# Split weights kept in DRAM for their second use, and an output stage whose transposes and projection share three PSUM tiles

## The chip, the cores and the metric

The kernel runs on one core of one Trainium2 chip. The metric is the device time of one execution in microseconds (us), the median of three runs. The core has five engines that the text names: TensorE (PE, with its weight loads as PEld), VectorE (DVE), ScalarE (ACT), GpSimd (POOL) and SyncE (SP). In this kernel SP issues every DMA, in one order. SBUF is the working memory on the chip, PSUM the memory that TensorE writes, DRAM the large memory behind the DMA engines.

## The reference, cut to what matters

One layer over 2048 tokens of width 1024. One projection of the normed input feeds three branches; each branch's output is multiplied by a gate, projected and merged with weights that are computed too.

```python
h = _layer_norm(x, ln_in_g, ln_in_b)
proj = h @ w_in[l]                       # 1024 x 7592
(a_q, a_k, a_v, a_gate, i_q, i_k, i_w, b_q, b_k, b_v, b_gate,
 c_q, c_gate, m_gate) = _split_cols(proj, IN_SPLITS)
# partial rotary embedding on a_q, a_k, i_q, i_k, b_q, b_k
o_a = _dsa_attention(a_q, a_k, a_v, i_q, i_k, i_w)     # top 256 keys by an indexer
y_a = (o_a * jax.nn.silu(a_gate)) @ w_proj_a[l]
o_b = _diff_attention(b_q, b_k, b_v, lam)
y_b = (o_b.reshape(bsz, seq, B_WIDTH) * jax.nn.silu(b_gate)) @ w_proj_b[l]
y_c = (o_c.reshape(bsz, seq, C_WIDTH) * jax.nn.silu(c_gate)) @ w_proj_c[l]   # o_c: attention into mem
g = jax.nn.sigmoid(m_gate.reshape(bsz, seq, N_BRANCH, D_MODEL))
merged = g[:, :, 0] * y_a + g[:, :, 1] * y_b + g[:, :, 2] * y_c
h = _layer_norm(DEEPNORM_ALPHA * h + merged @ w_out[l], ln_g[l], ln_b[l])
```

## The kernel before, in words

**Three products for one.** Every large product is made of three (`mm3`, L76 to L79): both operands are split into a rounded part H and the rest L, and TensorE adds H by H (L77), H by L (L78) and L by H (L79) in PSUM. `split` (L67 to L74) makes the parts: a copy into the rounded type, on GpSimd (L69) or ScalarE (L71), then a subtraction (L74) on GpSimd or VectorE.

**Two halves.** The 2048 tokens are 16 blocks of 128. The transposed, split input of 8 blocks (a half) fits into SBUF at a time, in `H4`. `save_hT` stores half 0's to DRAM (`ht_d`, four stores of 2 MB), and `reload` brings it back when half 1 is through. So every column group of `w_in` is needed twice, once for each half.

**The weights.** `load_win` (L227) loads 256 columns of `w_in` in raw pieces `wr` of 256 KB (L235; four for a group, two of 512 KB for the very first) and splits each piece into the tile `w` of 2 MB, of which there are two. `dense` (L240) and `gate_steps` (L253) call it, so it runs once for each half. `dense_ai01` (L266) does the same for 424 columns in two tiles; its copies are ScalarE's in half 0 and GpSimd's in half 1.

**The order in time.** Half 0: `aq`, `ai`, a first top-k over blocks 2 to 7 beside `bk`, `bv` and `bq`; its end runs into half 1's products. Then half 1's input, `aq`, `ai`, two more top-k groups, `bk`, `bv`, `bq`, and all 20 gate jobs (`JOBS`, L378) of half 1. H is reloaded; half 0's gate jobs follow: four at once, twelve spread as filler through the second attention (four heads of 16 blocks, keys `kg`, values `vg`, queries `bq`), four after it, beside the memory tokens' products. The first attention, the mixing of branches two and three, and the output stage come behind that.

**Work beside the weights.** GpSimd does the rotary steps (L138 to L141, on `do`, the copied product) and, at the end of a top-k group, a comparison for each block (L576, tile `ja`), on which VectorE's chain of scans (L579 to L582) waits. Both stand in GpSimd's order among the weight splits. SP issues raw pieces, stores of products and loads in one order; a DMA that has to wait for an engine holds up all behind it. Apart from a few places written out by hand, the order of each engine is set by a scheduler when the kernel is built.

**The output stage.** `stage1` (L1032) takes pairs of blocks. `gated` (L925) loads the gate `ys` (L927), transposes the first branch's output on TensorE into PSUM `gT` (L930), multiplies it by the gate on VectorE (L932), copies it on ScalarE (L933) and subtracts on GpSimd (L934). `branch` (L937) makes the projection from it, four PSUM tiles `yps` for a pair, which VectorE multiplies into `ft` (L943). `gT` has one PSUM tile, `yps` two, `ys` one buffer. The output projection (`fz`) runs between.

Of the kernel before, what the change touches and what calls it, by code (L numbers as in the profile page):

```python
# [58 lines left out]
def tile_layer(ctx, tc, x, mem, ln_in_g, ln_in_b, w_in, w_mem_kv, diff_lambda, diff_norm_g,  # L59
# [23 lines left out]
    def dram(name, shape, dt=F32):  # L83
        return dr.tile(shape, dt, name=name)
# [20 lines left out]
    mg_d = [dram(f"mg_d{p}", [128, KT, 256]) for p in range(NP)]  # L105

# [120 lines left out]
    def load_win(cols, eh=G, el=G, rpool=None):  # L227
        w = dw.tile([128, 2, KT, 256], F32R, name="w")
        n = sum(c for _, c in cols)
        m = 2 if rpool is None else 4  # L230
        for i in range(0, KT, m):
            raw = (rpool or dw).tile([128, m, 256], F32, name="wr", bufs=2)
            o0 = 0
            for c0, cn in cols:
                SP.dma_start(raw[:, :, o0:o0 + cn], w_view(w_in, i * 128, m, c0, cn))  # L235
                o0 += cn
            split(w[:, 0, i:i + m, :n], w[:, 1, i:i + m, :n], raw[:, :, :n], eh, el)
        return w
# [27 lines left out]
    def dense_ai01(half):  # L266
        W = []
        for i in range(2):
# [5 lines left out]
            W.append(w)  # L274
            for c0, cols in ((0, [(C_AK, 128), (C_IQ, 128)]), (256, [(C_IQ + 128, W_AI - 256)])):
                n = sum(c for _, c in cols)
                for k in (0, 2):
                    raw = dw.tile([128, 2, 256], F32, name="wr", bufs=2)
                    o0 = 0
                    for a0, an in cols:  # L280
                        SP.dma_start(raw[:, :, o0:o0 + an], w_view(w_in, i * 512 + k * 128, 2, a0, an))
                        o0 += an
                    split(w[:, 0, k:k + 2, c0:c0 + n], w[:, 1, k:k + 2, c0:c0 + n], raw[:, :, :n], A if half == 0 else G, G)
# [641 lines left out]
    def gated(pool, psp, pname, o, s, r, b, oT):  # L925
        t = slice(128 * (b % 2), 128 * (b % 2) + 128)
        SP.dma_start(s, sg_d[r][b // 4][:, :, 128 * (b % 4):128 * (b % 4) + 128])  # L927
        ps = psp.tile([128, 4, 128], F32, name=pname, bufs=2 if pname == "cps" else 1)
# [7 lines left out]
    def branch(psp, w, oT, u, t, bufs):  # L936
        y = psp.tile([128, 2, 256], F32, name="yps", bufs=bufs)  # L937
# [73 lines left out]
    for p in range(NP):  # L1011
        T = []
        for r, w, mix in ((1, wb, gated_b), (2, wc, gated_c)):
            oT = yp.tile([128, 2, 4, 256], F32R, name="yoT")
            mix(p, oT)
            for u in range(4):
# [3 lines left out]
                branch(yq, w, oT, u, t, 1)  # L1020
# [12 lines left out]
    def stage1(p, acc):  # L1033
        oT = fs.tile([128, 2, 4, 256], F32R, name="yoT")
        for b in (2 * p, 2 * p + 1):
            o = fs.tile([128, 512], F32, name="fo")
            SP.dma_start(o, oa_d[b])
            gated(fs, fqr, "gT", o, fs.tile([128, 4, 128], F32, name="ys", bufs=1), 0, b, oT)
        for u in range(4):
# [3 lines left out]
            branch(fqr, wa, oT, u, t, 2)  # L1043
# [129 lines left out]
```

## Time and profile before

| what | before |
| --- | --- |
| median of 3 runs | 2956.33 us (2955.36 to 2962.07) |
| profiled execution | 2954.62 us, of which 2952.8 are the span |
| TensorE busy | 2785.7 us (94%) |
| VectorE busy | 2130.6 us (72%) |
| ScalarE busy | 1398.0 us (47%) |
| GpSimd busy | 1140.0 us (39%) |
| moved by DMA | 383.09 MB, mean 130 GB/s |
| mean granted clock of TensorE | 0.980 |

The profiled execution is one of its own and not among the three. The span runs from the first to the last instruction. A share of busy time is a mean over the whole span; where an engine is short of work is seen in the stretches, and why in the waits. In rows of the trace, times are us from the start of the span; `out<-in` are the names of the tiles, and a bracket at a row's end is the idle time of the engine before it, with what ended it.

### The profile page before, as it was taken

What the parts mean: (1) busy time and instruction counts of PE and PEld (TensorE: products, weight loads), DVE (VectorE), ACT (ScalarE), POOL (GpSimd) and SP (SyncE); (2) the same over time, 40 slices, a digit from 0 to 9 for tenths busy, and PEclk for the clock granted to TensorE, in tenths of its full rate; (3) what the DMA queues carried; (4) which work ended last, traced back from release to release, by engine and by line L of the source; (5) the groups of instructions that cost most, each with busy time, mean ns of one, the idle gap of its engine ahead of it and who ended that gap; (6) DMA issues with size and microseconds to landing.
All of it is one profiled execution on the core that took longest, in us unless ns stands there. A gap on an engine that the chain in (4) does not pass through costs nothing.

```text
span 2952.8 us, 49447 instructions
## 1 busy us (share of the span) xinstructions
PE 2785.7 (94%) x17488; PEld 2494.6 (84%) x17488; DVE 2130.6 (72%) x4885; ACT 1398.0 (47%) x2716; POOL 1140.0 (39%) x1510
## 2 busy tenths in 40 slices
PE   6999989999999988999999998998999999987998
PEld 6899989987888867787888887897999899977887
DVE  7189988999668997577777773447777777774555
ACT  3266645773346860344444442436555655552010
POOL 7554566435433328344444435231222222211232
PEclk9999999999999999999999999999999999998999
DMA  9454444342322364433333325235333333358542
GB/s 341 134 149 143 148 121 136 119 144 93 115 86 84 95 196 143 134 96 104 107 109 96 109 68 153 71 98 185 101 104 98 116 111 110 116 169 271 185 146 83
DMA packets 357111, 383.09 MB, mean 130 GB/s; under 512 B 29952, under 2 KB 285312, under 8 KB 356352
## 3 DMA queue, kind: packets, MB, share of 16 engines
q1 hardware_dynamic: 356864, 379.94, 41.6%
q8 instruction: 138, 2.26, 0.3%
q14 instruction: 109, 0.89, 0.1%
HBM read 240.15 MB, written 139.69 MB: 129 GB/s over the span
## 4 chain that ended last, share of the span: by engine, by line
PE 57%; DVE 12%; DMA 6%; issue 5%; POOL 4%; ACT 3%; SPq 1%; DVEq 0%; POOLq 0%; ACTq 0%
PE dps L77 6%; PE dps L78 6%; PE dps L79 6%; PE ops L741 4%; DVE jd L531 4%; PE aops L886 4%; PE apt L881 3%; PE lg L636 3%; PE lg L637 3%; PE yps L78 3%; PE yps L77 3%; PE yps L79 3%; PE pt L749 2%; PE fz L79 2%; PE fz L78 2%
## 5 line engine op out<-in xcount | busy, mean ns | idle before, releaser
L77 PE MATMUL dps<-H,w 128*128 128x512 f32 x1280 | 519.3, 406 | 26.1 <-DMA H<-ht_d 8.1
L78 PE MATMUL dps<-H,w 128*128 128x512 f32 x1280 | 504.8, 394 | 0.0
L79 PE MATMUL dps<-H,w 128*128 128x512 f32 x1280 | 503.8, 394 | 0.9 <-POOL w L74 0.9
L69 POOL TENSOR_SCALAR w<-wr 128x512 fp32r<-128x512 f32 x240 | 184.9, 778 | 591.7 <-PE dps L79 449.7
L74 POOL TENSOR_TENSOR w<-wr,w 128x512 fp32r<-128x512 f32 (+2 forms) x254 | 361.1, 1431 | 17.2 <-ACT w L71 11.0
L77 PE MATMUL dps<-w,H 128*128 128x256 f32 (+1 forms) x1152 | 341.9, 298 | 12.9 <-POOL w L69 5.7
L544 ACT ACTIVATE ja<-sall,thr 128x1280 bf16<-128x1280 f32 (+4 forms) x224 | 302.1, 1348 | 109.0 <-DVE thr L540 99.1
L78 PE MATMUL dps<-w,H 128*128 128x256 f32 (+1 forms) x1152 | 342.8, 298 | 4.1 <-POOL w L74 4.1
L79 PE MATMUL dps<-w,H 128*128 128x256 f32 (+1 forms) x1152 | 341.4, 297 | 2.2 <-DVE H L74 2.2
L531 DVE TENSOR_SCALAR_CACHE_REDUCE jd<-sall,thr 128x1408 bf16<-128x1408 f32 (+6 forms) x231 | 330.9, 1433 | 6.4
L77 PEld LDWEIGHTS dps<-H,w 128*128 128x128 f32 x1280 | 243.4, 190 | 72.6 <-issue 13.9
L79 PEld LDWEIGHTS dps<-H,w 128*128 128x128 f32 x1280 | 242.6, 190 | 53.2 <-POOL w L74 1.8
L78 PEld LDWEIGHTS dps<-H,w 128*128 128x128 f32 x1280 | 244.1, 191 | 37.6
L639 DVE CUSTOM_DVE_ANT_0 AP<-lg,bias 128x512 f32<-128x512 f32 (+3 forms) x304 | 181.8, 619 | 124.6 <-PE lg L637 60.6
L504 DVE SCALAR_TENSOR_TENSOR sall<-ir,iw,sall 128x512 f32<-128x512 f32 (+3 forms) x266 | 212.8, 852 | 57.9 <-ACT ir L500 56.4
L77 PEld LDWEIGHTS dps<-w,H 128*128 128x128 f32 x1152 | 224.0, 195 | 16.4 <-POOL w L69 6.2
L71 ACT CAST apr<-apt 128x512 fp32r<-128x512 f32 (+1 forms) x288 | 157.5, 562 | 159.8 <-PE apt L881 128.3
L78 PEld LDWEIGHTS dps<-w,H 128*128 128x128 f32 x1152 | 224.5, 195 | 6.5 <-POOL w L74 5.8
L77 PE MATMUL yps<-yoT,H 128*128 128x256 f32 x768 | 223.5, 293 | 4.5 <-DVE ft L943 3.9
L74 DVE TENSOR_TENSOR apr<-apt,apr 128x512 fp32r<-128x512 f32 (+1 forms) x288 | 185.6, 656 | 58.2 <-ACT apr L71 56.4
L79 PEld LDWEIGHTS dps<-w,H 128*128 128x128 f32 x1152 | 224.3, 195 | 3.5 <-DVE H L74 2.6
L886 PE MATMUL aops<-apr,VA 128*128 128x256 f32 x1088 | 208.8, 299 | 16.9 <-ACT apr L71 6.7
(244 smaller groups left out, 6820.2 us busy)
## 6 DMA issues: line engine op xcount, KB each, us to landing
wr<-in_w_in_dram SPq DMA_DIRECT2D x220, 256.0 KB, 3.0
tm_d<-do SPq DMA_DIRECT2D x96, 256.0 KB, 2.1
bq<-qb_d SPq DMA_DIRECT2D x128, 128.0 KB, 3.3
aq<-qa_d SPq DMA_DIRECT2D x128, 128.0 KB, 3.2
yt<-tm_d SPq DMA_DIRECT2D x64, 256.0 KB, 3.1
sg_d<-do SPq DMA_DIRECT2D x48, 256.0 KB, 2.5
ys<-sg_d SPq DMA_DIRECT2D x48, 256.0 KB, 3.5
facc<-mg_d SPq DMA_DIRECT2D x48, 256.0 KB, 4.7
```

What stands on the lines that cost most here:

```text
L69: G.tensor_scalar(H, src, 1.0, 1.0, op0=ALU.mult, op1=ALU.mult)
L71: A.copy(H, src)
L74: el.tensor_tensor(L, src, H.bitcast(F32), op=ALU.subtract)
L77: PE.matmul(ps, lH, rH, start=start, stop=False)
L78: PE.matmul(ps, lH, rL, start=False, stop=False)
L79: PE.matmul(ps, lL, rH, start=False, stop=stop)
L504: V.scalar_tensor_tensor(s[:, c0:c0 + cn], r[:, :cn], iw[:, h:h + 1], s[:, c0:c0 + cn], op0=ALU.mult, op1=ALU.add)
L531: V.tensor_scalar(jd[:, :L], sc[b], t.bitcast(F32)[:, i:i + 1], None, op0=op, op1=ALU.add, accum_out=dst[:, i:i + 1])
L544: A.activation(ja[:, :L], sc[b], AF.Sign, bias=thr.bitcast(F32)[:, i:i + 1], scale=-1.0, accum_out=cnt[:, i:i + 1])
L639: V.tensor_tensor_reduce(P[:, c0:c0 + cn], ps[:, :cn], bias[:, c0:c0 + cn], scale=-0.125, scalar=-LOW, op0=ALU.add, op1=ALU.min, accum_out ...
L741: PE.matmul(o_ps.rearrange("p a d -> p (a d)"), pr[:, a, i], v, start=(k0 + i == 0 and a == 0), stop=(k0 + i == b and a == 1))
L886: PE.matmul(o_ps.rearrange("p a d -> p (a d)"), VA[:, k0 + i], pr[:, a, i].rearrange("p e q -> p (e q)"), start=(k0 + i == 0 and a == 0), ...
```

## The change

`load_win` keeps a table `w_d` by the first column of its group. On the first use the tile is made as before and then stored whole, with one DMA of 2 MB, to a DRAM tensor of its own. On the second use the tile is filled from there by one DMA of 2 MB; there are no raw pieces and no split. `dense_ai01` does this for its two tiles (1.7 MB each, stored in half 0, loaded in half 1). In the output stage `gT` and the projection's `yps` become one name with three PSUM tiles in turn, and `ys` has two buffers.

```diff
--- before.py
+++ after.py
@@ -103,6 +103,7 @@
     oa_d = [dram(f"oa_d{b}", [128, 512]) for b in range(NB)]
     ob_d = [dram(f"ob_d{b}", [128, 512]) for b in range(NB)]
     mg_d = [dram(f"mg_d{p}", [128, KT, 256]) for p in range(NP)]
+    w_d = {}
 
     const = ctx.enter_context(tc.tile_pool(name="const", bufs=1))
     idf = const.tile([128, 128], F32, name="idf")
@@ -226,6 +227,10 @@
 
     def load_win(cols, eh=G, el=G, rpool=None):
         w = dw.tile([128, 2, KT, 256], F32R, name="w")
+        key = cols[0][0]
+        if key in w_d:
+            SP.dma_start(w.bitcast(F32), w_d[key])
+            return w
         n = sum(c for _, c in cols)
         m = 2 if rpool is None else 4
         for i in range(0, KT, m):
@@ -235,6 +240,8 @@
                 SP.dma_start(raw[:, :, o0:o0 + cn], w_view(w_in, i * 128, m, c0, cn))
                 o0 += cn
             split(w[:, 0, i:i + m, :n], w[:, 1, i:i + m, :n], raw[:, :, :n], eh, el)
+        w_d[key] = dram(f"w_d{key}", [128, 2, KT, 256])
+        SP.dma_start(w_d[key], w.bitcast(F32))
         return w
 
     def dense(kind, half, cols, idx, w=None):
@@ -272,6 +279,9 @@
                 w = dw.tile([128, 2, KT, 256], F32R, name="w")
                 w = w.rearrange("p a k c -> p (a k c)")[:, :8 * W_AI].rearrange("p (a k c) -> p a k c", a=2, k=4)
             W.append(w)
+            if half:
+                SP.dma_start(w.bitcast(F32), w_d["ai", i])
+                continue
             for c0, cols in ((0, [(C_AK, 128), (C_IQ, 128)]), (256, [(C_IQ + 128, W_AI - 256)])):
                 n = sum(c for _, c in cols)
                 for k in (0, 2):
@@ -280,7 +290,9 @@
                     for a0, an in cols:
                         SP.dma_start(raw[:, :, o0:o0 + an], w_view(w_in, i * 512 + k * 128, 2, a0, an))
                         o0 += an
-                    split(w[:, 0, k:k + 2, c0:c0 + n], w[:, 1, k:k + 2, c0:c0 + n], raw[:, :, :n], A if half == 0 else G, G)
+                    split(w[:, 0, k:k + 2, c0:c0 + n], w[:, 1, k:k + 2, c0:c0 + n], raw[:, :, :n], A, G)
+            w_d["ai", i] = dram(f"w_dai{i}", [128, 2, 4, W_AI])
+            SP.dma_start(w_d["ai", i], w.bitcast(F32))
         for p in range(4 * half, 4 * half + 4):
             ps = [dqs.tile([128, 512], F32, name="dps") for _ in range(2)]
             for a in range(2):
@@ -925,7 +937,7 @@
     def gated(pool, psp, pname, o, s, r, b, oT):
         t = slice(128 * (b % 2), 128 * (b % 2) + 128)
         SP.dma_start(s, sg_d[r][b // 4][:, :, 128 * (b % 4):128 * (b % 4) + 128])
-        ps = psp.tile([128, 4, 128], F32, name=pname, bufs=2 if pname == "cps" else 1)
+        ps = psp.tile([128, 4, 128], F32, name=pname, bufs=2 if pname == "cps" else 3)
         for c in range(4):
             PE.transpose(ps[:, c], o[:, c * 128:(c + 1) * 128], idf)
         with tc.high_priority():
@@ -933,8 +945,8 @@
             A.copy(oT[:, 0, :, t], s)
             G.tensor_tensor(oT[:, 1, :, t], s, oT[:, 0, :, t].bitcast(F32), op=ALU.subtract)
 
-    def branch(psp, w, oT, u, t, bufs):
-        y = psp.tile([128, 2, 256], F32, name="yps", bufs=bufs)
+    def branch(psp, w, oT, u, t, name, bufs):
+        y = psp.tile([128, 2, 256], F32, name=name, bufs=bufs)
         for i in range(2):
             c = slice(256 * u + 128 * i, 256 * u + 128 * i + 128)
             for k in range(4):
@@ -1017,7 +1029,7 @@
                 t = yw.tile([128, 2, 256], F32, name="yt")
                 T.append(t)
                 SP.dma_start(t, tm_d[r][p // 2][:, 2 * u:2 * u + 2, 256 * (p % 2):256 * (p % 2) + 256])
-                branch(yq, w, oT, u, t, 1)
+                branch(yq, w, oT, u, t, "yps", 1)
         for u in range(4):
             G.tensor_tensor(T[u], T[u], T[4 + u], op=ALU.add)
             SP.dma_start(mg_d[p][:, 2 * u:2 * u + 2], T[u])
@@ -1035,12 +1047,12 @@
         for b in (2 * p, 2 * p + 1):
             o = fs.tile([128, 512], F32, name="fo")
             SP.dma_start(o, oa_d[b])
-            gated(fs, fqr, "gT", o, fs.tile([128, 4, 128], F32, name="ys", bufs=1), 0, b, oT)
+            gated(fs, fqr, "gT", o, fs.tile([128, 4, 128], F32, name="ys"), 0, b, oT)
         for u in range(4):
             t = fs.tile([128, 2, 256], F32, name="ft")
             SP.dma_start(t, tm_d[0][p // 2][:, 2 * u:2 * u + 2, 256 * (p % 2):256 * (p % 2) + 256])
             SP.dma_start(acc[u], mg_d[p][:, 2 * u:2 * u + 2])
-            branch(fqr, wa, oT, u, t, 2)
+            branch(fqr, wa, oT, u, t, "gT", 3)
             V.tensor_tensor(acc[u], acc[u], t, op=ALU.add)
 
     def accs(ap, bufs):
```

The lines of the changed program are some 12 further down than those of before behind this. In SP's order these are the pieces of ai's first and second tile in half 0, among stores of `aq` products (`qa_d`). Before:

```order
L225 DMA qa_d_0_85<-de 128x4x256
L281 DMA wr<-in_w_in_dram 128x2x168 x2
L225 DMA qa_d_1_86<-de 128x4x256
L225 DMA qa_d_2_87<-de 128x4x256
L225 DMA qa_d_3_88<-de 128x4x256
L281 DMA wr<-in_w_in_dram 128x2x128 x4
L281 DMA wr<-in_w_in_dram 128x2x168 x2
L235 DMA wr<-in_w_in_dram 128x2x256 x4
```

With the change (`w_dai` and `w_d` are the kept weights):

```order
L226 DMA qa_d_1_86<-de 128x4x256
L291 DMA wr<-in_w_in_dram 128x2x168
L226 DMA qa_d_2_87<-de 128x4x256
L226 DMA qa_d_3_88<-de 128x4x256
L291 DMA wr<-in_w_in_dram 128x2x128 x2
L295 DMA w_dai_1097<-w 128x3392
L291 DMA wr<-in_w_in_dram 128x2x128 x2
L291 DMA wr<-in_w_in_dram 128x2x168 x2
L240 DMA wr<-in_w_in_dram 128x2x256
L295 DMA w_dai_1118<-w_1099 128x3392
L240 DMA wr<-in_w_in_dram 128x2x256 x2
```

Stores of 1.7 MB (L295) stand between the pieces of the second ai tile and ahead of most pieces of the next group. Next, GpSimd at the end of the first top-k group (blocks 2 to 7, which runs into half 1's products), from the comparison of 128x640 on; `w<-wr` are weight splits, `rt` and `do` rotary steps. Before:

```order
L576 TENSOR_SCALAR ja<-sall,tf 128x640
L140 TENSOR_TENSOR do<-do,rp 128x2x16
L140 TENSOR_TENSOR do<-do,rp 128x2x4x8
L69 TENSOR_SCALAR w<-wr 128x512
L141 TENSOR_TENSOR do<-do,rt 128x2x16
L141 TENSOR_TENSOR do<-do,rt 128x2x4x8
L74 TENSOR_TENSOR w<-wr,w 128x512
L69 TENSOR_SCALAR w<-wr 128x512
L138 TENSOR_TENSOR rt<-do,rp 128x10x4
L139 TENSOR_TENSOR rt<-do,rp 128x10x4
```

With the change, around the same comparison (L588):

```order
L141 TENSOR_TENSOR do<-do,rp 128x2x5x8
L142 TENSOR_TENSOR do<-do,rt 128x2x5x8
L588 TENSOR_SCALAR ja<-sall,tf 128x640
L139 TENSOR_TENSOR rt<-do,rp 128x8x8
L140 TENSOR_TENSOR rt<-do,rp 128x8x8
L141 TENSOR_TENSOR do<-do,rp 128x8x16
L142 TENSOR_TENSOR do<-do,rt 128x8x16
```

The weight copies and subtractions are gone from between, and rotary steps stand next to each other. Last, TensorE in the output stage, at a change of pair; `fo` is a block's output, `H_257` holds the projection's weights. Before, there are three of one block's four transposes in the middle of the pair's products:

```order
L78 MATMUL yps<-yoT,H_257 128x256
L79 MATMUL yps<-yoT,H_257 128x256
L930 MATMUL gT<-idf,fo 128x128 x3
L77 MATMUL yps<-yoT,H_257 128x256
L78 MATMUL yps<-yoT,H_257 128x256
```

With the change, at the end of the same pair's products, which now write into `gT`:

```order
L78 MATMUL gT<-yoT,H_257 128x256
L79 MATMUL gT<-yoT,H_257 128x256
L942 MATMUL gT<-idf,fo 128x128 x8
L77 MATMUL gT<-yoT,H_257 128x256 x2
L78 MATMUL gT<-yoT,H_257 128x256
L79 MATMUL gT<-yoT,H_257 128x256
```

All eight transposes of the next pair stand together, directly ahead of the products that read them.

## Rows read from the trace of the kernel before

**Rows 1.** The page: busy time by engine, and the chain that ended last.
```profile
PE 2785.7 (94%) x17488; PEld 2494.6 (84%) x17488; DVE 2130.6 (72%) x4885; ACT 1398.0 (47%) x2716; POOL 1140.0 (39%) x1510
...
PE 57%; DVE 12%; DMA 6%; issue 5%; POOL 4%; ACT 3%; SPq 1%; DVEq 0%; POOLq 0%; ACTq 0%
```

**Rows 2.** Stretches: their length, busy us (instructions) by engine, clock, DMA share, GB/s.
```profile
core 0: us, PE busy (x) PEld busy (x) DVE busy (x) ACT busy (x) POOL busy (x), PEclk, DMA share, GB/s
20.00:80.00 60.00, 49.54 (x382) 48.01 (x381) 41.66 (x60) 22.06 (x34) 50.32 (x58) 0.94 0.96 336
400.00:500.00 100.00, 86.16 (x621) 83.66 (x620) 82.87 (x151) 38.01 (x86) 72.20 (x89) 0.93 0.44 130
550.00:700.00 150.00, 149.70 (x883) 132.89 (x882) 141.66 (x265) 113.10 (x161) 60.60 (x84) 1.00 0.39 126
1078.00:1104.00 26.00, 17.87 (x72) 14.08 (x71) 22.76 (x43) 13.82 (x18) 3.65 (x4) 0.87 1.09 355
1100.00:1150.00 50.00, 41.45 (x162) 32.42 (x161) 41.48 (x35) 4.10 (x7) 42.08 (x18) 0.91 0.46 153
1800.00:1850.00 50.00, 40.28 (x175) 31.51 (x175) 11.70 (x33) 10.88 (x22) 20.40 (x33) 0.90 0.55 172
2615.00:2720.00 105.00, 81.11 (x499) 72.42 (x497) 53.86 (x129) 35.21 (x84) 12.77 (x9) 0.87 0.74 238
```

**Rows 3.** The page's groups: weight splits; busy us, mean ns, idle before them, releaser.
```profile
L69 POOL TENSOR_SCALAR w<-wr 128x512 fp32r<-128x512 f32 x240 | 184.9, 778 | 591.7 <-PE dps L79 449.7
L74 POOL TENSOR_TENSOR w<-wr,w 128x512 fp32r<-128x512 f32 (+2 forms) x254 | 361.1, 1431 | 17.2 <-ACT w L71 11.0
```

**Rows 4.** TensorE's waits from 400 to 460: us, times, longest.
```profile
PE psT L218 <- POOL do L141: 6.7, 3, 3.2
PE dps L78 <- POOL w L74: 3.7, 3, 1.8
PE dps L77 <- POOL w L69: 3.4, 1, 3.4
```

**Rows 5.** Timeline of GpSimd from 414: start us, us, line.
```profile
414.59 1.56 POOL L576 TENSOR_SCALAR ja<-sall,tf 128x512 bf16<-128x512 f32 x1 [2.26 <-DVE pf L582]
416.12 2.10 POOL L69 TENSOR_SCALAR w<-wr 128x512 fp32r<-128x512 f32 x2
418.19 3.15 POOL L74 TENSOR_TENSOR w<-wr,w 128x512 fp32r<-128x512 f32 x2
```

**Rows 6.** Waits of TensorE and of its weight loads from 1080 to 1150.
```profile
PE dps L77 <- DVE do L309: 5.3, 2, 2.9
...
PEld dps L77 <- DVE need L578: 3.4, 1, 3.4
PEld dps L77 <- POOL w L69: 3.3, 1, 3.3
```

**Rows 7.** The page's DMA issues: count, KB each, median us to landing.
```profile
wr<-in_w_in_dram SPq DMA_DIRECT2D x220, 256.0 KB, 3.0
```

**Rows 8.** Timelines of SP and of ScalarE where ai's pieces are issued and split.
```profile
64.77 4.08 SPq L281 DMA_DIRECT2D wr<-in_w_in_dram  x3
...
81.20 0.59 ACT L333 COPY do<-dps 128x512 f32<-128x512 f32 x1 [5.61 <-PE dps L79]
81.68 1.14 ACT L71 CAST w<-wr 128x512 fp32r<-128x512 f32 x2
```

**Rows 9.** TensorE's waits from 80 to 115.
```profile
PE dps L77 <- ACT w L71: 3.4, 2, 2.4
```

**Rows 10.** TensorE's waits from 1200 to 1800, for the keys at changes of head.
```profile
PE lg L636 <- DMA kg<-kb_d: 4.4, 2, 2.5
...
PE lgx L636 <- DMA kg<-kb_d: 3.2, 1, 3.2
```

**Rows 11.** TensorE's waits from 2615 to 2720.
```profile
PE gT L930 <- DVE ys L932: 13.0, 4, 9.0
```

**Rows 12.** Timelines of SP and of VectorE at the longest of these.
```profile
2675.26 0.53 SPq L927 DMA_DIRECT2D ys<-sg_d  x1
...
2682.67 0.69 DVE L932 SCALAR_TENSOR_TENSOR ys<-gT,ys 128x512 f32<-128x512 f32 x1 [0.83 <-DMA ys<-sg_d]
```

**Rows 13.** The subtraction on tile `ys` from 2600 to 2730: ns min/median/max.
```profile
L934 POOL TENSOR_TENSOR yoT<-ys,yoT x9: 1267/1294/1732, 2631.0 to 2726.0; 128x512 fp32r<-128x512 f32 x9
```

## The prediction

> **What bounds the kernel now.** I read the page's busy line first: TensorE works for 2785.7 of 2952.8 us, the next engine, VectorE, for 2130.6, GpSimd for 1140.0 [rows 1]. Most of the time is matmuls that this change leaves alone, and a faster GpSimd is worth nothing as such: at most TensorE's idle 167 us (2952.8 - 2785.7), and what the clock loses around idle spots, can come back. The chain that ended last agrees: TensorE 57%, VectorE 12%, DMA 6%, GpSimd 4% [rows 1]. GpSimd's 4% is some 118 us, but a step of that chain is often replaced at once by its neighbour, so it is a ceiling and no forecast.
>
> Then I read where TensorE is short of work, in the table by stretches [rows 2]. From 550 to 700 us, where the gate products of half 1 run, it is busy for 149.70 of 150 at full clock: the split weights are there in time, although GpSimd makes all of them. The groups say with how much slack: the 240 copies of L69 waited 449.7 us for TensorE to give back a weight buffer [rows 3]. In such stretches the second use is hidden already. The poor ones are few: 20 to 80 us, 400 to 500, 1050 to 1150, 1800 to 1850 and 2615 to 2720. The change touches all five.
>
> **Part 1, what it takes away.** The second use of 28 tiles loses four copies (0.778 us) and four subtractions (1.431) each, 28 x 4 x 2.209 = 247 us of GpSimd [rows 3]; the two tiles of `dense_ai01(1)` lose 16 instructions more. It pays where GpSimd has other work that TensorE waits for.
>
> *400 to 500 us* (the first products of half 1 beside the end of the first top-k; GpSimd is busy for 72.20 of 100). TensorE loses 100 - 86.16 = 13.8 us, and the clock stands at 0.93, which over 100 us is another 7 [rows 2]: 21. What ends the waits is GpSimd: 6.7 us for the rotary step `do` (L141), 3.7 for L74, 3.4 for L69, together also 13.8 [rows 4]. The timeline shows why: at 414.59 the top-k comparison (1.56), then two copies (2.10) and two subtractions (3.15), and the rotary steps only behind those [rows 5]. In the order of the change no weight step stands there, so a rotary step waits for a comparison at most. I give back the 13.8 and half of the clock's 7: 17.
>
> The new price is the whole tile. GpSimd has the buffer at 416.12 and is through with the first two pieces at 418.19 + 3.15 = 421.3 [rows 5]. After the change a load of 2 MB stands there. The reload of H moves its 2 MB loads at 355 GB/s [rows 2], 5.9 us each; a lone 256 KB piece takes 3.0 [rows 7], of which 0.7 is that rate, so 2.3 lie around it: 8.2, whole at 424. That is 3 to 7 us of wait, once; I take 5. Term: -17 + 5 = **-12**, from -20 (no price, nothing else late) to -4 (the rotary steps stay late behind comparisons and VectorE, the tile costs 7).
>
> The Trainium skill, "Perfetto Trace Analysis", section "DMA Optimizations", says that splitting DMAs into smaller chunks may let some of the work start sooner, which speaks against one 2 MB load in place of four pieces. By that rule alone the tile would cost its full 7 and the term be -10. The rows at 416 to 421 show the pieces held by GpSimd for 5 us anyway, so I let the rows decide; no run here shows a second load in pieces.
>
> *1050 to 1150 us.* TensorE first waits through the reload of H: busy for 17.87 of 26 at a clock of 0.87 [rows 2]. It releases that buffer itself, and the change leaves this. Then come waits of 3.3 us for L69, 3.4 for `need` and 5.3 for `do`, both VectorE's [rows 6], while GpSimd is busy for 42.08 of 50 [rows 2] with splits between four long comparisons. In the order of the change the four comparisons stand one behind another. The 3.3 go; VectorE's chain of scans stays but starts sooner, so I take half of the other 8.7, no clock, and give back 2 for a 2 MB load ahead of H's. -3.3 - 4.3 + 2 is about **-6**, from -12 (all waits) to 0 (VectorE's scans set all of it).
>
> **Part 1, what it adds.** 28 stores of 2 MB, 2 of 1.7, and as many loads in place of 30 MB of raw pieces: some 60 MB more written, 30 more read, over 2952.8 us. Three stretches count.
>
> *20 to 110 us.* The DMA engines are busy for 0.96 of 20 to 80 us [rows 2], so each store of 2 MB pushes what stands behind it by 5.9. Two of them (the first tile's ahead of the first `ht_d`, the second tile's between the pieces for ai) make 12. ScalarE took those pieces at 81.68, right behind a copy for which it had waited on TensorE; they had been issued until 68.9 [rows 8], and at about twice a piece's 3.0 us they lay there by 72 to 75. So 7 to 10 of cover against 12: 2 to 5 late, I take 3. The first ai store (4.9) then stands between the pieces of the second ai tile, for whose split TensorE waits already (3.4 in two waits [rows 9]): 3 late. Term **+6**, from +2 (one of the two is covered after all) to +14 (12 + 5 with a fifth covered).
>
> *110 to 1050 us.* 26 stores beside matmuls that leave the DMA at 0.39 to 0.44 [rows 2]. SP has to wait for the subtractions before it issues a store, and the gates' stores and top-k's loads behind it wait too; the slack of [rows 3] covers most. **+2**, from 0 to +12 (a dozen places with one us).
>
> *1200 to 1800 us*, twelve gate jobs as filler in the second attention. The splits that vanish were hidden. What can suffer are the short loads when the head changes, for which TensorE waits 7.6 us today, in three waits [rows 10]: SP's order now has 2 MB loads among them, one directly ahead of the first `kg` piece. One such load, 5.9, less the four pieces that leave (3.0 at the rate), less 1 for GpSimd's other steps: **+2**, from -6 (most of the 7.6 vanish) to +15 (5.9 at all three, less 3).
>
> *1800 to 1850 us.* TensorE loses 9.7 us with GpSimd at 20.40 of 50 and the DMA at 0.55 [rows 2]; its first work there hangs on loads. SP no longer waits on GpSimd for the weights ahead of these. **-2**, from -5 to +4.
>
> **Part 2, the output stage.** From 2615 to 2720 TensorE is busy for 81.11 of 105 us at a clock of 0.87 [rows 2]. Of its waits, 13.0 us in four are transposes held up by L932, the longest 9.0 [rows 11]: with a single `ys` buffer its load is issued only at 2675.26, and the step runs at 2682.67 [rows 12]. With two buffers that load goes out a block ahead, and the 9.0 vanish. The ring of three costs something: transposes that were strewn among the products (three, then five) now stand eight in a row just ahead of the products that need them. Behind the last come 0.69 (L932), 0.62 (a copy, from the same engine as `de`'s, 0.59 [rows 8]) and 1.29 for the second operand (L934 [rows 13]); with the other block's steps beside them some 2.8 bare, at two changes of pair 5.6, in place of the other waits' 4.0. So -9.0 + 1.6 = -7.4; I take **-6**, since the DMA is at 0.74 and 238 GB/s over the stretch [rows 2] and other loads may come last in its place. From -15 (clock and all) to +8 (the 9.0 come back as a wait for another load, the 5.6 stand on top, and the clock adds 2).
>
> **The sum.** +6 + 2 - 12 - 6 + 2 - 2 - 6 = -16. Against the profiled execution, 2954.6, that is 2938.6; that execution lies 1.7 below the median of the three runs, 2956.33, from which the sum gives **2940 us**. A measurement of this kernel can tell about 0.3%, 8.9 us, from no change.
>
> **The rivals.**
> *Nothing gained*, 2948 to 2964. The second use was hidden, as from 550 to 700, and from 400 to 500 the rotary steps stay late behind comparisons and VectorE: that term is -4, the one at 1100 is 0, the other five make +2: 2956 - 2 = 2954. For it: GpSimd's 449.7 us of waiting for TensorE [rows 3]. Against it: GpSimd is named in all the waits of [rows 4].
> *Slower: 2 MB pieces in one queue.* Short transfers stand behind long ones in SP's order, and the three DMA terms come out at their upper ends: 14 + 12 + 15 = 41 in place of 10, so 2940 + 31 = 2971. It decides from the point where the push exceeds the cover: more than the 7 to 10 us for the early pieces, more than the 3 us of pieces saved when a head changes. For it: 0.96 early. Against it: about 0.4 elsewhere [rows 2].
> *The larger gain*, 2905 to 2930. GpSimd's stalls take the clock's loss along: -20, -12 and -15 in place of -24 together, thus 2940 - 23 = 2917. For it: 0.93, 0.91 and 0.87 of the clock just where TensorE is idle [rows 2]. Against it: something else is late next in all three, above all VectorE.
>
> **How the numbers follow.** Forecast (2931 to 2947) 0.42, nothing gained 0.25, slower 0.15, larger gain 0.18. Faster by over 0.3% are the forecast and the larger gain, 0.60; within it 0.25; slower 0.15. For 8 in 10 I leave out the slower rival and the lower part of the larger gain: 2918 to 2963.
>
> **What would show it.** From 400 to 500 no wait for L69 or L74, those for L141 under 3 us, one of about 5 for the DMA of `w`, busy there up from 86 to about 95. From 1100 to 1150 no wait for weights. From 80 to 115 waits for ai's weights of some 9, not 3.4. In the output stage no 9 us wait, but two of 2 to 3. If the idle time from 400 to 500 keeps its size under VectorE's name, part 1 was hidden; if waits for `kg` pass 15 us, the queue rival is right; if the output stage stays at 81 of 105 under DMA names, my reading of part 2 is wrong.

## The result, and the profile after

The changed kernel takes 2921.88 us (median of four runs, 2919.38 to 2925.13) against 2958.89 of before in the same comparison (four runs, 2955.36 to 2962.07): a ratio of 0.9885, 95% interval 0.9863 to 0.9907. That is 1.15% faster, 34 to 37 us, against 16 forecast. The time lies inside the stated range, near its lower end, where the prediction had put the larger gain and not its own forecast. The profiled execution after took 2925.13 us, 29.5 less than that of before.

The page of the changed kernel, busy time by engine and the chain that ended last:

```profile
PE 2778.1 (95%) x17488; PEld 2490.2 (85%) x17488; DVE 2053.1 (70%) x4885; ACT 1401.7 (48%) x2716; POOL 864.6 (30%) x1270
...
HBM read 271.25 MB, written 201.88 MB: 162 GB/s over the span
...
PE 68%; DMA 7%; DVE 6%; issue 3%; POOL 2%; ACT 2%; SPq 1%; POOLq 0%; DVEq 0%; ACTq 0%
```

GpSimd does 275 us less than in [rows 1], as costed (247 and `dense_ai01`'s part). What the prediction did not expect is VectorE: the same 4885 instructions, none of them changed by part 1, take 77 us less. VectorE's share of the chain falls from 12% to 6%, which alone would prove little: in `pieces` below, which is as fast as the change, it is 12% again.

The stretches that answer to [rows 2] (the columns are the same; 300 to 400 is new; the last two begin 22 and 23 us earlier, as far as the program is ahead there, and the last is 100 long, not 105):

```profile
20.00:80.00 60.00, 49.79 (x374) 47.79 (x372) 43.20 (x60) 22.17 (x34) 50.36 (x58) 0.94 1.05 374
300.00:400.00 100.00, 97.40 (x741) 95.59 (x740) 88.97 (x213) 73.03 (x156) 35.34 (x81) 1.00 0.52 173
400.00:500.00 100.00, 94.87 (x733) 93.35 (x733) 72.61 (x156) 40.51 (x92) 39.16 (x62) 0.97 0.58 195
550.00:700.00 150.00, 148.86 (x816) 128.95 (x816) 140.17 (x258) 110.22 (x156) 55.49 (x76) 1.00 0.59 204
1100.00:1150.00 50.00, 48.78 (x214) 39.59 (x213) 38.95 (x39) 5.33 (x9) 19.83 (x4) 1.00 0.57 199
1778.00:1828.00 50.00, 41.38 (x185) 32.74 (x184) 11.25 (x35) 11.04 (x24) 13.14 (x25) 0.93 0.62 193
2592.00:2692.00 100.00, 82.55 (x524) 72.91 (x522) 54.15 (x130) 34.88 (x84) 12.42 (x9) 0.90 0.78 245
```

From 400 to 500 TensorE is busy for 94.87 in place of 86.16, with GpSimd at 39.16 in place of 72.20 and the clock up from 0.93 to 0.97. From 1100 to 1150 it is 48.78 in place of 41.45 (part of that is the reload of H, which lies a little earlier now). The waits that answer to [rows 4] (from 400 to 470), [rows 9] (from 80 to 115), and [rows 10] (from 1180 to 1790):

```profile
PE dps L77 <- DMA w<-w_d: 2.6, 1, 2.6
PE psT L219 <- POOL do L142: 2.4, 1, 2.4
...
PE dps L77 <- ACT w L71: 8.6, 2, 5.2
...
PE lg L648 <- DMA kg<-kb_d: 5.1, 2, 3.2
...
PE lgx L648 <- DMA kg<-kb_d: 1.8, 1, 1.8
```

The waits for L69 and L74 are gone, the one for the whole tile came (2.6, forecast 5), the one for ai's weights grew from 3.4 to 8.6 (forecast 9), and the keys are waited for as long as before (6.9 against 7.6).

**Where the 29.5 us were won.** To compare places although the order of the matmuls differs, I added up the columns of TensorE's matmuls over each trace (a transpose's twice, since they take about twice as long) and read off the time at which a given share of them was done. The table is worked out that way; it shows us later (+) or earlier (-) than the profiled execution of before at the same share. The shares are rounded; in before they lie at 147, 372, 502, 1018, 1141, 1256, 1788, 2574, 2724 and 2945 us.

```
share of TensorE's columns   4%   11%    15%    34%    38%    42%    61%    88%    92%   all
the change                  7.4   1.6  -14.1  -11.8  -22.2  -21.9  -22.0  -22.4  -32.9 -29.5
p1_weights                  8.4   4.3  -12.0   -8.2  -18.0  -16.8  -19.6  -21.8  -18.2 -18.6
p2_output                   0.1  -2.0   -2.7    2.5    2.0    0.7    3.4    5.2   -8.9  -5.3
p2_ys                      -1.0  -3.4   -5.5   -5.5   -3.8   -4.9   -0.5    2.0   -5.1  -3.9
p2_ring                    -0.8  -5.8   -7.9   -6.5   -6.3   -8.1   -6.4   -5.2    5.1   6.2
stores_only                 8.3   9.5    9.7   19.1    8.7   19.5   21.7   26.4   27.0  27.8
dummy_splits                7.2   4.2   -5.4   -0.5   -6.0   -0.8    5.6    1.3  -12.0 -11.5
keep_dense                  7.7   2.0  -13.5   -7.1  -21.6   -3.5   -3.9   -4.6    1.4   1.0
keep_gates                 -0.9  -4.6   -5.8    1.2   -5.9   -9.0   -9.5  -12.4  -24.5 -19.4
keep_no_aq                  2.0   0.5  -12.9  -11.6  -20.8  -19.9  -20.3  -23.0  -35.5 -31.9
keep_no_early               0.8   1.4  -11.5  -11.0  -24.2  -25.9  -26.0  -24.3  -36.8 -34.8
```

How far such a table goes is seen in the three kernels that change the output stage alone (`p2_`): up to that stage the order of their instructions is the same as before's on each engine, and yet they stand between 8 us ahead and 5 behind. A difference of one profile under some 8 us is therefore not explained here; what a kernel is worth is read from its ratio. What a kernel wins between two neighbouring points is told more finely: from 11% to 15% these three move by at most 2.1 us, from 34% to 42% by at most 1.8, while from 42% to 88% they fall back by 3 to 7. The points at 38% and 92% lie where TensorE waits, so that a slightly other share there reads up to 5 us otherwise; differences are better read past them.

### The profile page after: what moved, and what is told of

Its sections match the earlier page's. It is cut to its first block, busy times and chain, and to the rows that moved or that the text cites. A ratio compares the mean times of both kernels' runs of the same rounds, so it can differ in the third digit from the quotient of the medians.

```text
span 2923.3 us, 49093 instructions
## 1 busy us (share of the span) xinstructions
PE 2778.1 (95%) x17488; PEld 2490.2 (85%) x17488; DVE 2053.1 (70%) x4885; ACT 1401.7 (48%) x2716; POOL 864.6 (30%) x1270
## 4 chain that ended last, share of the span: by engine, by line
PE 68%; DMA 7%; DVE 6%; issue 3%; POOL 2%; ACT 2%; SPq 1%; POOLq 0%; DVEq 0%; ACTq 0%
PE dps L77 9%; PE dps L78 9%; PE dps L79 9%; PE ops L753 4%; PE aops L898 4%; PE apt L893 3%; PE lg L648 3%; PE lg L649 3%; PE yps L77 2%; PE yps L78 2%; PE yps L79 2%; PE pt L761 2%; PE fz L77 2%; PE fz L78 2%; PE fz L79 2%
## 5 line engine op out<-in xcount | busy, mean ns | idle before, releaser
L516 DVE SCALAR_TENSOR_TENSOR sall<-ir,iw,sall 128x512 f32<-128x512 f32 (+3 forms) x266 | 191.9, 768 | 70.6 <-ACT ir L512 68.1
L74 DVE TENSOR_TENSOR apr<-apt,apr 128x512 fp32r<-128x512 f32 (+1 forms) x288 | 185.5, 656 | 57.1 <-ACT apr L71 55.4
L69 POOL TENSOR_SCALAR w<-wr 128x512 fp32r<-128x512 f32 x120 | 87.1, 734 | 424.7 <-PE dps L79 339.2
L885 ACT ACTIVATE AP<-AP,anm 128x1024 f32<-128x1024 f32 (+7 forms) x192 | 172.1, 900 | 67.7 <-DVE anm L882 64.1
L512 ACT ACTIVATE ir<-ips 128x512 f32<-128x512 f32 (+3 forms) x304 | 150.0, 550 | 105.4 <-PE ips L507 92.0
```

The source lines that it names most:

```text
L74: el.tensor_tensor(L, src, H.bitcast(F32), op=ALU.subtract)
L512: A.activation(r[:, :cn], ps[:, :cn], AF.Relu)
L516: V.scalar_tensor_tensor(s[:, c0:c0 + cn], r[:, :cn], iw[:, h:h + 1], s[:, c0:c0 + cn], op0=ALU.mult, op1=ALU.add)
L885: A.activation(p[:, c0:c1], p[:, c0:c1], AF.Exp, bias=nm[:, e:e + 1], scale=-1.0, accum_out=sm[:, hd, i:i + 1])
```

## The experiments

All ratios are to the kernel before, on the same chip, with 95% intervals.

**p1_weights and p2_output: one part alone.** The edits are the two halves of the change's diff: in `p1_weights` the lines of `gated`, `branch` and `stage1` are those of before, in `p2_output` those of `load_win` and `dense_ai01`.

> The kept weights alone, with the output stage of before. Theory (GpSimd's second splits were what the products of half 1 waited for): about 22 us below before (2936), since in the two traces TensorE's products stand 22 us earlier at 2570 us and the rest of the gain comes behind that. Rival (the two parts help each other, the output stage being late anyway): under 15 us.

> The output stage alone, weights split twice as before. Theory: 7 us below before (2951), from the 9 us wait at ys that goes and some 2 us of transposes that stand bare. Rival (the gain there came with the earlier start): within 2 us of before.

Measured: 0.9925 (0.9910 to 0.9940), 2933.8 us, and 0.9966 (0.9954 to 0.9978), 2944.7 us. The two add up to the change: 0.75% and 0.34% against 1.15%. So 22 us belong to the weights and 10 to the output stage; neither needs the other.

**p2_ys and p2_ring: the output stage taken apart.**

```diff
# p2_ys, from the kernel before
-            gated(fs, fqr, "gT", o, fs.tile([128, 4, 128], F32, name="ys", bufs=1), 0, b, oT)
+            gated(fs, fqr, "gT", o, fs.tile([128, 4, 128], F32, name="ys"), 0, b, oT)
# p2_ring, from the kernel before
-        ps = psp.tile([128, 4, 128], F32, name=pname, bufs=2 if pname == "cps" else 1)
+        ps = psp.tile([128, 4, 128], F32, name=pname, bufs=2 if pname == "cps" else 3)
...
-            branch(fqr, wa, oT, u, t, 2)
+            branch(fqr, wa, oT, u, t, "gT", 3)
```

> Before with nothing but the second ys buffer in the output stage. Theory (the 9 us wait at the single buffer is all of part 2's gain, and the shared PSUM tiles cost a little): 9 to 11 below before, as much as part 2 whole. Rival (one gT tile holds the transposes back anyway): under 4 below before.

> Before with nothing but the three PSUM tiles shared by the transposes and the projection. Theory (the wait at the single ys buffer stays): within 2 of before, or 2 above for the bare transposes. Rival (with three tiles the transposes come earlier, and ys is asked for earlier): 5 or more below before.

Measured: the second `ys` buffer alone 0.9972 (0.9958 to 0.9986), the shared tiles alone 1.0021 (1.0006 to 1.0035). The gain is the buffer's. The shared tiles alone lose some 6 us (2 to 10 by the interval), because eight transposes in a row need both blocks' gates at once, and the single buffer gives the second only when the first is done. TensorE's waits from 2560 to 2740, first of `p2_ring`, with SP's and VectorE's rows at its longest, then of `p2_ys`, last of the change:

```profile
PE gT L77 <- ACT yoT L933: 17.2, 3, 12.7
...
2656.62 0.75 SPq L927 DMA_DIRECT2D ys<-sg_d  x1
...
2663.52 0.69 DVE L932 SCALAR_TENSOR_TENSOR ys<-gT,ys 128x512 f32<-128x512 f32 x1 [10.26 <-DMA ys<-sg_d]
...
PE gT L930 <- DVE ys L932: 3.6, 1, 3.6
PE gT L930 <- DMA fo<-oa_d: 3.5, 2, 2.9
...
PE gT L942 <- DVE ft L955: 4.5, 1, 4.5
...
PE gT L77 <- ACT yoT L945: 1.8, 2, 1.5
...
PE gT L78 <- POOL yoT L946: 1.6, 2, 0.9
```

In `p2_ring` the 9.0 of [rows 11] has become 12.7 behind the same buffer: the eight transposes are through by 2652.2, the second block's gate is asked for at 2656.62 and multiplied at 2663.52. In the change it is gone, and 4.5 for a PSUM tile of the ring and 3.4 of bare steps stand in its place. With the buffer doubled, the ring's own effect is not to be told from nothing (0.9966 with it, 0.9972 without).

**stores_only: the price of keeping.** Every first use stores its tile (the two of ai likewise, not shown in the cut), nobody reads the stores, the second use is that of before.

```diff
+        if key not in w_d:
+            w_d[key] = dram(f"w_d{key}", [128, 2, KT, 256])
+            SP.dma_start(w_d[key], w.bitcast(F32))
         return w
```

> Before with the 30 stores of split weights added and never read: second use still loads raw pieces and splits. Theory: the stores cost 7 us in the first 150 us (ai's pieces late) and nothing later, so 7 above before. Rival (stores also delay the short transfers later on): 15 or more above before.

Measured: 1.0080 (1.0062 to 1.0097), 24 us more. The rival was right. 8 us come in the first 150, as the prediction had it; most of the rest (9.7 to 19.1 in the table) comes between 500 and 1020, where the gates' tiles are stored, at single places. The last store goes out at 1065; what the profile loses from 42% to 88%, 6.9 us, is no more than what the three `p2_` kernels lose there. The largest single place is a stall of TensorE of 7.4 us at 759. The timelines of SP and of VectorE there:

```profile
750.64 0.32 SPq L242 DMA_DIRECT2D w_d<-w  x1
751.06 0.37 SPq L325 DMA_DIRECT2D sg_d<-do  x1
751.48 0.93 SPq L237 DMA_DIRECT2D wr<-in_w_in_dram  x1
752.83 0.92 SPq L591 DMA_DIRECT2D bias_d<-pf  x1
...
762.03 4.20 DVE L587 TENSOR_TENSOR_SCAN pf<-ones,ja 128x1536 f16<-128x1536 bf16 x1 [8.51 <-DMA bias_d<-pf]
766.15 0.66 DVE L324 SCALAR_TENSOR_TENSOR do<-do,dps 128x512 f32<-128x512 f32 x1
```

The 2 MB store goes out at 750.64. The store of top-k's result, issued 2.2 us behind it, frees its buffer only when VectorE has waited 8.51 us for it, the next scan of 4.20 follows, and the gate's last step (L324), which frees the PSUM tile for TensorE, stands behind the scan. Here the short store landed 9.1 us after its issue. The other 13 of its kind in this run, none issued while a 2 MB transfer was under way, took 1.7 to 4.1. In the change five of the 14 are issued during such a transfer and take 3.4 to 9.8, the other nine 1.8 to 4.5. So in these traces a short transfer that meets one of 2 MB is late by up to some 7 us, about what a 2 MB store takes to land (7.3 in the median), and here it is the end of a chain over two engines. TensorE's waits from 690 to 1250, first of `stores_only`, then of the change:

```profile
PE dps L77 <- DVE do L324: 16.2, 5, 7.4
PE dps L77 <- DMA H<-ht_d: 5.7, 2, 5.5
PE dps L77 <- DVE need L586: 3.8, 3, 2.0
...
PE dps L77 <- DVE need L590: 5.1, 2, 4.4
PE dps L77 <- DVE do L328: 5.0, 4, 1.7
PE dps L77 <- DMA H<-ht_d: 4.6, 1, 4.6
```

**dummy_splits: the work without its result.** The second use loads the kept tile as in the change, but GpSimd still does the eight steps for each tile of `load_win` (not for ai's two), into a scratch buffer.

```diff
             SP.dma_start(w.bitcast(F32), w_d[key])
+            for i in range(0, KT, 2):
+                raw = dw.tile([128, 2, 256], F32, name="wr", bufs=2)
+                src = w[:, 0, i:i + 2].bitcast(F32)
+                G.tensor_scalar(raw.bitcast(F32R), src, 1.0, 1.0, op0=ALU.mult, op1=ALU.mult)
+                G.tensor_tensor(raw.bitcast(F32R), src, raw, op=ALU.subtract)
             return w
```

> The change, but at each second use of load_win's tiles GpSimd still does four copies and four subtractions of 128x512, from the loaded tile into a scratch buffer that nobody reads. Theory (rotary steps, top-k comparisons and VectorE's scans were late behind the splits on GpSimd, and TensorE behind them): most of the gain of part 1 is lost, 20 or more above the change. Rival (TensorE waited for the weights themselves, or SP for the raw buffers): within 8 of the change.

Measured: 0.9965 (0.9953 to 0.9978), 2946.8 us: what the output stage is worth alone (0.9966), and nothing more. The theory held, more fully than expected: with GpSimd's work in place, nothing is left of the gain of part 1, although no product waits for a split any more. Where TensorE waits instead, from 300 to 1230, first in the change, then in `dummy_splits` (rotary steps, then VectorE's top-k and gate steps, whose lines are 5 further down in the second):

```profile
PE psT L219 <- POOL do L142: 3.0, 2, 2.4
PE dps L77 <- DVE need L590: 5.1, 2, 4.4
PE dps L77 <- DVE do L321: 3.6, 3, 2.9
PE dps L77 <- DVE do L328: 5.7, 5, 1.7
...
PE psT L219 <- POOL do L142: 8.3, 8, 2.4
PE dps L77 <- DVE need L595: 7.5, 3, 3.2
PE dps L77 <- DVE do L326: 6.8, 4, 3.1
PE dps L77 <- DVE do L333: 6.9, 5, 2.2
```

All of TensorE's waits there (those over 0.15 us) add up to 51.5 us in before, 32.8 in the change and 51.0 in `dummy_splits`. TensorE, VectorE and GpSimd in the two stretches where GpSimd is busiest beside top-k, of before, of the change, of `dummy_splits` (busy us in the order TensorE, weight loads, VectorE, ScalarE, GpSimd):

```profile
300.00:480.00 180.00, 159.19 (x1139) 153.74 (x1137) 155.51 (x328) 92.94 (x207) 119.19 (x176) 0.95 0.45 137
1100.00:1230.00 130.00, 116.34 (x487) 93.14 (x486) 80.32 (x101) 18.32 (x27) 76.08 (x40) 0.95 0.52 157
...
300.00:480.00 180.00, 172.27 (x1304) 168.94 (x1303) 144.80 (x337) 99.62 (x218) 73.92 (x142) 0.98 0.55 183
1100.00:1230.00 130.00, 120.70 (x553) 98.96 (x552) 83.31 (x153) 26.68 (x39) 22.26 (x11) 0.96 0.58 187
...
300.00:480.00 180.00, 166.30 (x1249) 162.58 (x1247) 151.89 (x326) 95.37 (x208) 115.02 (x175) 0.98 0.53 177
1100.00:1230.00 130.00, 107.98 (x455) 86.23 (x453) 84.71 (x118) 19.57 (x29) 78.31 (x44) 0.95 0.54 174
```

From 300 to 480 the load in place of the split brings part of the gain (159 to 166, where the `p2_` kernels stand at 160 to 164), the relief of GpSimd the rest (166 to 172). From 1100 to 1230 the dummy work puts TensorE below before. In the table `dummy_splits` wins nothing from 34% to 42% (-0.5 to -0.8), where the change wins 10.1.

**keep_dense and keep_gates: which tiles.** The table is filled only for the ten tiles of aq, ai, bk, bv and bq, or only for the gates' 20; the others are split twice.

```diff
# keep_dense
+        if C_AQ <= key < C_AK or C_BQ <= key < C_BG:
             w_d[key] = dram(f"w_d{key}", [128, 2, KT, 256])
             SP.dma_start(w_d[key], w.bitcast(F32))
# keep_gates: dense_ai01 as before, and
+        if C_AG <= key < C_IQ or key >= C_BG:
             w_d[key] = dram(f"w_d{key}", [128, 2, KT, 256])
             SP.dma_start(w_d[key], w.bitcast(F32))
```

> The change with only the ten tiles of aq, ai, bk, bv and bq kept; the gates' weights are split twice as before. Theory (the gain lies from 300 to 470 us, where the gates are not yet running): 8 to 10 above the change, that is 26 below before. Rival (GpSimd's load as a whole counts, and the gates are 20 of 30 tiles): 20 above the change or more.

> The change with only the gates' 20 tiles kept; aq, ai, bk, bv and bq are loaded raw and split twice as before. Theory after the first runs (each place is worth what its own waits were): no store ahead of 150 us, so 8 given back there; 4 lost again from 300 to 390 and 16 from 390 to 470; the gates' 18 up to 1810 us and the output stage's 7 stay. About 25 below before, 10 above the change. Rival (the places hang together, and the start of the gates decides): 10 or less below before.

Measured: `keep_dense` 1.0006 (0.9997 to 1.0016), so nothing is left of 34 us, although the output stage's 10 are in this kernel too; its theory (26 below before) was wrong, the rival's number right. `keep_gates` 0.9922 (0.9898 to 0.9945), 23 us below, as its theory had it. In the table `keep_dense` has the whole gain at 15% (-13.5). From 34% to 42% it loses 3.6 us where the change wins 10.1, and one wait of 11.7 makes most of that difference. It is the first of these, from 1100 to 1250:

```profile
PE lg L649 <- DMA bq<-qb_d: 11.7, 1, 11.7
PE dps L77 <- DVE need L591: 4.5, 2, 3.0
```

and what SP waited for just ahead of it, from 1130 to 1205:

```profile
SPq L240 <- POOL w L74: 21.7, 8, 8.8
SPq L330 <- DVE do L329: 6.6, 2, 6.4
```

The first queries of the second attention stand in SP's line behind raw pieces, and those wait for GpSimd to split the pieces ahead of them while it does the four long comparisons. Kept tiles of the gates take such waits out of SP's line. But in before SP waits no less for L74 (25.2 us from 1130 to 1205), and TensorE does not wait for `bq` at all: it takes the order in SP's line as well, and no run separates the two. So the tiles' gains do not simply add, and an order that the scheduler happens to choose can be worth more than 10 us. It loses 5 us more in the output stage, where its order differs from the change's; that part was not followed up.

**g_stores and pieces: other ways to move the tiles.**

```diff
# g_stores (both places)
-        SP.dma_start(w_d[key], w.bitcast(F32))
+        G.dma_start(w_d[key], w.bitcast(F32))
# pieces
-            SP.dma_start(w.bitcast(F32), w_d[key])
+            for i in range(0, KT, 2):
+                SP.dma_start(w[:, :, i:i + 2].bitcast(F32), w_d[key][:, :, i:i + 2])
```

> The change with the 30 stores of split weights issued by GpSimd, which has just done the last subtraction, in place of SP. Theory (the stores cost because SP stands waiting for the split, and short transfers behind it): 10 below the change. Rival one (it is the traffic): within 4 of the change. Rival two (issuing costs GpSimd more than SP): above the change.

> The change with each second load in four DMAs of 512 KB in place of one of 2 MB. Theory (a tile's first piece comes 5 us sooner, which counts in the one place where the tile is late, at 420 us): 2 to 4 below the change. Rival (four issues in place of one lengthen SP's line): 3 or more above it.

Measured: 0.9927 (0.9904 to 0.9951) and 0.9896 (0.9876 to 0.9916). Stores from GpSimd are not the 10 us better that was expected, and by the middle of the interval 12 us worse than the change. Why is not shown: they land in 8.4 us in place of 7.3, and GpSimd is busy for 876.8 in place of 864.6. The four pieces are the same as one load, the range of either holds the other. The Trainium skill, "Perfetto Trace Analysis", section "DMA Optimizations", says that smaller DMAs may let some of the work start sooner; here the wait from 400 to 470 was 2.6 us in one for the whole tile and 3.9 us in three for the pieces, so the trace does not bear it out in the one place where it was expected to tell.

**keep_no_aq and keep_no_early: without the early stores.**

```diff
# keep_no_aq (and ai's stores issued behind the first products of ai)
+        if key >= C_AK:
             w_d[key] = dram(f"w_d{key}", [128, 2, KT, 256])
             SP.dma_start(w_d[key], w.bitcast(F32))
# keep_no_early: the same condition, and dense_ai01 as before
```

> The change without keeping aq's two tiles (they are loaded raw and split twice as before), and with ai's two stores issued behind the first products of ai. Theory (the two 2 MB stores in the saturated first 80 us cost, aq's kept tiles give back nothing): 4 of the first 7 us come back and nothing is lost, 4 below the change, ratio to before about 0.987. Rival (aq's second splits were in the way from 330 to 400): 3 above the change.

> The change without keeping aq's and ai's tiles; bk, bv, bq and the gates stay kept. Theory (ai's second splits stand among the top-k comparisons and rotary steps from 380 to 420, so they carry some of the 16 us won there): all of the first 7 us come back, but 6 to 10 of the 16 are lost; within 4 of the change. Rival (only the b tiles count there): 7 below the change.

Measured: 0.9897 (0.9878 to 0.9916) and 0.9879 (0.9863 to 0.9895), 2919.2 us. Neither can be told from the change (0.9885); the 4 us below it that `keep_no_aq` was expected to give did not come. In the table, of the 7.4 us at 4% some 5 are gone in `keep_no_aq` and 7 in `keep_no_early`, as expected, and by 15% `keep_no_aq` and the change are level again. `keep_no_early` keeps four tiles fewer, was the fastest kernel that was run, and its profile (2918.3 us of span, clock 0.984) is 5 us below that of the change; with these intervals that is a hint and no more.

## Why the prediction was right in sign and too small

It held the direction, the places of part 2 and of the early stores, and the range. By its own steps:

| step | forecast | shown |
| --- | --- | --- |
| stores from 20 to 110 us | +6 | +7.4 (change), +8.3 (`stores_only`), -0.9 and +0.8 without these stores |
| stores from 110 to 1050 us | +2 (0 to 12) | +10.8 in `stores_only` between 4% and 34%; in the change what is left beside the relief is +2.3 between 15% and 34% |
| 147 to 372 us | no term | -5.8 between 4% and 11%, but -2.1 to -5.0 in the `p2_` kernels too, which change nothing there |
| 400 to 500 us | -12 | -15.7 between 11% and 15% of the columns |
| 1050 to 1150 us | -6 | -10.1 between 34% and 42%; +0.4 in `stores_only`, -0.3 in `dummy_splits` |
| second attention | +2 | nothing (-21.9 to -22.0); waits for `kg` 6.9 against 7.6 |
| 1800 to 1850 us | -2 | -2.0 at 1850 us, read like the table; -0.4 between 61% and 88% (the `p2_` kernels move by as much) |
| output stage | -6 | -7 in the profile, 0.9966 alone, that is 10 |

**The step that failed** is the sentence that a faster GpSimd is worth nothing as such, and with it the way in which the relief was costed: by the waits that name GpSimd, in two places. Three amounts of about 0.8% each stand behind the net 0.75% of part 1; the first was measured by itself, the other two are differences between kernels whose orders differ too. Storing costs 0.8% (`stores_only`). Loading a finished tile in place of pieces and a split gives 0.8% back, since `dummy_splits`, which pays for the stores and has no relief, comes out at the output stage's 0.9966 again. The relief of GpSimd itself gives the last 0.8%, the distance from `dummy_splits` (0.9965) to the change (0.9885), whose intervals do not touch. The prediction had +8 for the first (24 measured), and -18 for the second and third together (-12 - 6 + 2 - 2; some 46 measured). Both were too small by more than half, and the errors took each other away in part: the net of part 1, -10 in place of 22, is off by 12, its two terms by 16 and 28. That the time still fell into the range is in part luck of this kind.

Why were they too small? For the stores I took the waiting of L69 for TensorE [rows 3] as slack that covers them. It is slack of the weights; a 2 MB store ahead of top-k's short store holds up VectorE's next scan and TensorE behind it, as the row at 762 shows. For the relief I looked at the wait that ended last. [rows 4] names L69, L74 and the rotary steps; it does not show that VectorE's own steps, behind `need` and `do` in [rows 6], were stretched by GpSimd: from 1080 to 1150 those beside a GpSimd instruction took 8.1 us more in before than their kind takes without one, 0.0 in the change (1058 to 1128) and 7.5 in `dummy_splits` (1075 to 1145); how that was worked out stands in the last section.

**400 to 500 us** went as told: no wait for weights from GpSimd, the tile's own wait at 422 (2.6 in place of 5), the rotary wait at 2.4. The row at 416 had been read rightly. I had not looked at 300 to 400, where the second `aq` tiles are used: TensorE is busy for 93.03 of 100 there in the trace of before, 97.40 after, another 4 us; up to 95.62 in the `p2_` kernels, so that 2 of the 4 are clear of the difference between executions.

**The output stage** was the right mechanism; `p2_ys` and `p2_ring` confirm the buffer as its cause and the ring as no gain of its own. That the ring would cost 6 us without the second buffer, the sum did not contain.

**Nothing gained** fell with the ratio. **The queue rival** was right in its mechanism and wrong in its balance: the added stores do cost 24 us, but the change wins more by the loads in place of pieces and by GpSimd's relief than it pays. The keys at a change of head, where the prediction had placed this rival, were not touched. **The larger gain** is what came in size, and in part by its mechanism: at its three places the clock rose from 0.93, 0.91 and 0.87 to 0.97, 1.00 and 0.90, and the three brought -15.7, -10.1 and -7.1, between its -47 and the forecast's -24. Over the whole the clock is 0.982 against 0.980, and TensorE's busy time for the same 17488 matmuls fell by 7.6 of the 29.5 us. `dummy_splits` has that clock and busy time too (0.982, 2778.5) and not the gain, so the clock is not what separates the two.

**Left open:** how the relief's 22 us divide between rotary steps and comparisons that come sooner on GpSimd, and VectorE's steps that become shorter. In the table `dummy_splits` falls behind the change by 6.1 us from 11% to 15% and by 9.8 from 34% to 42%, clear of the 2 us that the `p2_` kernels move there, and by 6.5 from 42% to 61%, where those move by up to 4.4. Of the waits shown for 300 to 1230, those for rotary steps grow by 5.3 us and those for VectorE by 6.8; the latter hold both shorter steps and earlier comparisons. No kernel was run in which GpSimd is busy without touching the memory that VectorE uses.

## What to carry to other kernels

Slack that shows as an engine's waiting for another covers only that engine's own results; other work on the same queue, and short transfers behind long ones, may have none. To price a relief, ask which other engines run beside the relieved one, and test it with the work left in and its result unused: here that one run showed more than all waits. And when a ring of buffers is shared to let work run ahead, first look at every other buffer on that path; here one left single made the shared ring a loss.

## What the runs showed of the hardware

VectorE's steps are shorter when no GpSimd instruction runs beside them. The group of L504 (L516 and L521 in the other two), the same 266 instructions on the same shapes, of before, the change and `dummy_splits` (busy us, mean ns):

```profile
L504 DVE SCALAR_TENSOR_TENSOR sall<-ir,iw,sall 128x512 f32<-128x512 f32 (+3 forms) x266 | 212.8, 852 | 57.9 <-ACT ir L500 56.4
...
L516 DVE SCALAR_TENSOR_TENSOR sall<-ir,iw,sall 128x512 f32<-128x512 f32 (+3 forms) x266 | 191.9, 768 | 70.6 <-ACT ir L512 68.1
...
L521 DVE SCALAR_TENSOR_TENSOR sall<-ir,iw,sall 128x512 f32<-128x512 f32 (+3 forms) x266 | 200.2, 805 | 65.3 <-ACT ir L517 63.8
```

852 ns, 768 and 805, with GpSimd busy for 1140.0, 864.6 and 1115.6 us; VectorE as a whole goes 2130.6, 2053.1 and 2104.7. GpSimd's total is not what counts: `stores_only` has 808 ns with 1133.2 us, `keep_gates` 827 with 955.2, `keep_dense` 775 with 1045.4. What counts is which steps coincide. Worked out from the starts and ends in the traces, the group's 196 steps of 128x512 divide so:

| | with no GpSimd instruction beside them | with one |
| --- | --- | --- |
| before | 108, 745 ns in the mean | 88, 1121 ns |
| the change | 133, 747 ns | 63, 967 ns |
| `dummy_splits` | 119, 743 ns | 77, 1044 ns |

The same for all of VectorE, each step against the median of its kind without GpSimd (over all the runs, kinds with at least five such steps): those beside GpSimd take 152 us more in before, 75 in the change and 126 in `dummy_splits`; those without it differ by no more than about 3 us. The difference of 77 us is all that VectorE saves by the change.

The Trainium skill, "SBUF — State Buffer", section "SBUF: two separate sides", says that a VectorE operation with two inputs in SBUF and a GpSimd operation take turns on one pair of ports. This instruction has two such inputs, and the rows agree in direction; the share of it in the time of the kernel was not measured by itself.
